# The up-projection of a ConvFFN: seven products of sums of quarters in place of eight

## The chip, the cores and the metric

The kernel runs on one core of one Trainium2 chip. A core has a tensor engine (TensorE, PE in the profile; its weight loads are shown as PEld), a vector engine (VectorE, DVE), a scalar engine (ScalarE, ACT), a general engine (GpSimd, POOL) and a queue that issues most of the DMAs (SyncE, SP). Each works through its own list of instructions in order and waits on semaphores for the others. The metric is the device time of one execution in microseconds (us); less is better.

## The reference

One inference step of a two-layer trunk. 1024 prompt tokens and 8 sequences of 4 sample tokens go through each layer: three kinds of linear-attention heads (RWKV-7, GLA, retention) side by side, an output projection, a LayerNorm, a gated ConvFFN, a second LayerNorm. All in float32; the states are outputs too. The part that matters here:

```python
def _conv_ffn(x, conv0, w_up, conv_w, conv_b, w_down):      # D_MODEL 1024, D_FF 2816, CONV_W 3
    t_ = x.shape[1]
    u = x @ w_up                                            # 1024 -> 2 * 2816
    buf = jnp.concatenate([conv0.astype(u.dtype), u], axis=1)
    c = conv_b + sum(conv_w[j] * buf[:, j:j + t_] for j in range(CONV_W))
    a, b = jnp.split(c, 2, axis=-1)
    return (jax.nn.gelu(a) * b) @ w_down, buf[:, -(CONV_W - 1):]
...
        x = _layer_norm(ALPHA * x + mix, ln1_g[l], ln1_b[l])
        f, cv = _conv_ffn(x, s_conv[l], ffn_up[l], ffn_conv_w[l], ffn_conv_b[l], ffn_down[l])
        x = _layer_norm(ALPHA * x + f, ln2_g[l], ln2_b[l])
```

Each of the 5632 columns of `u` has its own filter over three tokens; a column of the first half, after a GELU, multiplies its partner in the second half.

## The kernel before, in words

Channels lie on the 128 partitions, tokens along the free axis. The 1056 tokens are three blocks (`NB`): 384 and 384 of the prompt, and a third of 288, which holds the 32 sample tokens and the last 256 of the prompt.

A product in float32 is made of three matmuls in the type float32r (`mm3`): every operand is split in a high part (a cast on ScalarE) and a low part (the rest, by a subtraction on GpSimd or VectorE), and high x high, high x low and low x high are added up in PSUM. `split` (L188) makes the two parts; all matmuls have line L128. Their order on TensorE is that of the program; on the other engines the framework's scheduler sets the order when the kernel is built, by priority and its own estimate of time.

In the FFN stage (L1355 to L1505) `x1` is the normed input, 8 tiles of 128 channels (k), in two parts, by block. The 2816 columns of each half make `NJ` = 22 tiles; `j` and `j + 22` belong together.

- `up(j)` takes both tiles, one after the other, over the three blocks. For each tile and block 8 k x 3 matmuls go to a PSUM bank `pu` (pool `pg`, 3 banks). `up_conv` then copies the bank to `u` in SBUF (L1380), with two columns of halo from the block before (L1376, L1378; GpSimd), starts `c` from the same bank on ScalarE (L1392) and adds two taps on VectorE (L1401). For the third block the samples, with their old state, are treated apart (L1384 to L1390).
- `up_gate` makes the GELU (L1406), the product (L1407) and its two parts `hh`, `hl` (L188).
- `up_blocks` is the same for j = 0 and j = 21, block by block.
- After two j (a pair) `downs` multiplies both with their rows of the down weights: for each block and each of 8 output tiles m, 2 x 3 matmuls to a bank `pd` (pool `pd`, 5 banks), which VectorE adds to `acc` in SBUF (L1448). The first two groups also bring in the residual, once for the high and once for the low part of `x1` (L1451).
- The last pair's downs go block by block (`last_downs`), with the sums of the second LayerNorm beside them; layer 0's blocks 1 and 2 are normed beside the next layer's first products.

Weights come in pieces of 128 x 512 (256 KB): a DMA on SP's queue to a raw tile `wr`, then `split` to `wh` and `wl`. The pool `wp` is open for the whole kernel: 4 raw tiles, and 4 of each part for the input, output and up-projection weights; the down weights' parts have 4 tiles each in the FFN's own pool. The constants `cs` are loaded once, at the start. `x1` of a block is read by `pu` until the last j.

## Time and profile before

| | |
|---|---|
| median of 3 runs | 3429.16 us (3426.34 to 3441.1) |
| span of the profiled execution | 3430.9 us, the time it is taken by here |
| TensorE busy | 3198.4 us (93%) |
| VectorE / ScalarE / GpSimd busy | 2068.6 / 1434.7 / 1332.6 us |
| mean granted clock of TensorE | 0.952 |
| FFN stage of layer 0, first `pu` to the start of the next layer's | 929.1 to 1705 us |
| FFN stage of layer 1 | 2624 to 3431 us |

In the profile's groups a row has the line, the engine, the operation, the tiles written and read (buffer numbers left out), their shapes, the count, then the busy time and the mean of one, then the idle time of the engine just before and what ended it. In a timeline a row has the start, the length, the engine, the line, the operation, and in brackets how long the engine had been idle and for whom it waited. "wU8h" is the high part of the up weights of tile 8, "wD8l" the low part of the down weights of j = 8.

### The profile page before, as it was taken

What the parts mean: (1) busy time and instruction counts of PE and PEld (TensorE: products, weight loads), DVE (VectorE), ACT (ScalarE), POOL (GpSimd) and SP (SyncE); (2) the same over time, 40 slices, a digit from 0 to 9 for tenths busy, and PEclk for the clock granted to TensorE, in tenths of its full rate; (3) what the DMA queues carried; (4) which work ended last, traced back from release to release, by engine and by line L of the source; (5) the groups of instructions that cost most, each with busy time, mean ns of one, the idle gap of its engine ahead of it and who ended that gap; (6) DMA issues with size and microseconds to landing.
All of it is one profiled execution on the core that took longest, in us unless ns stands there. A gap on an engine that the chain in (4) does not pass through costs nothing.

```text
span 3430.9 us, 59397 instructions
## 1 busy us (share of the span) xinstructions
PE 3198.4 (93%) x22110; PEld 2975.9 (87%) x22110; DVE 2068.6 (60%) x5037; ACT 1434.7 (42%) x3208; POOL 1332.6 (39%) x1660
## 2 busy tenths in 40 slices
PE   9889999988899999999888999999788999999995
PEld 8778888776799999999877888887777999999995
DVE  3577565776756544454746866646777564545457
ACT  6554332334543334333575543323346423333335
POOL 5443222224553334333565522221336433433345
PEclk9789999998999999999998999999989999999998
DMA  7333213433311111111154432234433111111111
GB/s 249 112 110 99 79 54 102 139 115 102 106 60 47 44 44 50 50 44 50 56 164 140 133 91 68 63 128 119 129 94 100 48 44 44 56 44 44 44 44 56
DMA packets 233261, 288.24 MB, mean 84 GB/s; under 512 B 65212, under 2 KB 146908, under 8 KB 232972
## 3 DMA queue, kind: packets, MB, share of 16 engines
q1 hardware_dynamic: 223852, 271.98, 26.3%
q10 hardware_dynamic: 9120, 12.47, 1.2%
q8 instruction: 173, 2.83, 0.4%
q14 instruction: 116, 0.95, 0.1%
HBM read 225.94 MB, written 58.43 MB: 83 GB/s over the span
## 4 chain that ended last, share of the span: by engine, by line
PE 70%; DVE 16%; DMA 4%; ACT 4%; issue 3%; POOL 2%; SPq 1%; ACTq 0%; DVEq 0%; POOLq 0%
PE pu L128 27%; PE pd L128 13%; PE gt L128 9%; PE pa L128 5%; PE po L128 3%; DVE tm L630 2%; DVE U L632 2%; PE zy L128 2%; PE gps L128 2%; PE rop L128 1%; DVE c L1401 1%; PE gop L128 1%; POOL wil L188 1%; DMA N<-gd 1%; DVE s L940 1%
## 5 line engine op out<-in xcount | busy, mean ns | idle before, releaser
L1401 DVE SCALAR_TENSOR_TENSOR c<-u,ppt,c 128x32 f32<-128x32 f32 (+1 forms) x704 | 395.8, 589 | 545.5 <-ACT c L1392 523.8
L188 POOL TENSOR_TENSOR wil<-wir,wih 128x512 fp32r<-128x512 f32 (+1 forms) x264 | 366.3, 1395 | 365.8 <-ACT wih L188 361.2
L128 PE MATMUL gt<-wih,xh 128*128 128x320 f32 (+1 forms) x1008 | 340.1, 339 | 0.9 <-DVE mx L388 0.9
L1448 DVE TENSOR_TENSOR acc<-acc,pd 128x384 f32<-128x384 f32 (+1 forms) x480 | 247.7, 518 | 139.5 <-PE pd L128 137.5
L128 PE MATMUL gt<-wil,xh 128*128 128x320 f32 (+1 forms) x1008 | 316.1, 315 | 6.5 <-POOL wil L188 5.2
L128 PE MATMUL gt<-wih,xl 128*128 128x320 f32 x896 | 281.6, 314 | 0.0
L188 ACT CAST wih<-wir 128x512 fp32r<-128x512 f32 (+1 forms) x296 | 185.6, 637 | 162.4 <-PE po L128 71.5
L128 PE MATMUL pa<-xh,wih 128*128 128x384 f32 (+1 forms) x576 | 216.5, 376 | 20.4 <-DVE mx L388 11.8
L630 DVE TENSOR_TENSOR tm<-U,N 96x60 f32<-96x60 f32 (+24 forms) x558 | 179.1, 321 | 69.9 <-DMA N<-gd 48.4
L128 PEld LDWEIGHTS gt<-wih,xh 128*128 128x128 f32 (+1 forms) x1008 | 187.5, 186 | 38.6 <-issue 21.9
L128 PE MATMUL pa<-xl,wih 128*128 128x384 f32 (+1 forms) x576 | 201.4, 350 | 3.3 <-POOL xl L188 3.0
L128 PE MATMUL pa<-xh,wil 128*128 128x384 f32 (+1 forms) x576 | 200.7, 348 | 3.6 <-POOL wil L188 2.2
L128 PEld LDWEIGHTS gt<-wil,xh 128*128 128x128 f32 (+1 forms) x1008 | 188.5, 187 | 10.2 <-POOL wil L188 9.1
L188 POOL TENSOR_TENSOR hl<-c,hh 128x384 fp32r<-128x384 f32 x132 | 128.1, 971 | 159.6 <-ACT hh L188 133.0
L632 DVE TENSOR_TENSOR U<-U,tm 96x60 f32<-96x60 f32 (+24 forms) x558 | 170.3, 305 | 14.0
L128 PEld LDWEIGHTS gt<-wih,xl 128*128 128x128 f32 x896 | 173.1, 193 | 0.0
L1392 ACT ACTIVATE c<-pu,ppt 128x384 f32<-128x384 f32 (+1 forms) x264 | 172.8, 655 | 0.0
L1380 ACT COPY u<-pu 128x384 f32<-128x384 f32 x176 | 84.1, 478 | 195.2 <-PE pu L128 195.1
L188 ACT CAST hh<-c 128x384 fp32r<-128x384 f32 x132 | 64.4, 488 | 222.4 <-DVE c L1407 222.3
L128 PEld LDWEIGHTS pa<-xh,wih 128*128 128x128 f32 x576 | 119.7, 208 | 35.1 <-DVE mx L388 13.2
L128 PE MATMUL po<-yh,wih 128*128 128x384 f32 (+1 forms) x384 | 138.9, 362 | 9.1 <-DVE ac L1325 6.7
L128 PE MATMUL po<-yh,wil 128*128 128x384 f32 (+1 forms) x384 | 131.7, 343 | 3.7 <-DVE wil L188 3.7
(810 smaller groups left out, 9862.6 us busy)
## 6 DMA issues: line engine op xcount, KB each, us to landing
wir<-in_wA_dram SPq DMA_DIRECT2D x144, 256.0 KB
wir<-in_wO_dram SPq DMA_DIRECT2D x96, 256.0 KB
wir<-in_wB_dram SPq DMA_DIRECT2D x56, 320.0 KB
tokd<-ev SPq DMA_DIRECT2D x112, 160.0 KB
x<-rkvd SPq DMA_DIRECT2D x16, 576.0 KB
tk<-tokd SPq DMA_DIRECT2D x16, 480.0 KB
rkvd<-mx SPq DMA_DIRECT2D x36, 192.0 KB
tk<-tokd SPq DMA_DIRECT2D x16, 400.0 KB
```

The costliest lines, as they stand in the source:

```text
L128: self.order(self.engine.matmul(out, lhsT, rhs, start=start, stop=stop), cols, 4 if rhs.dtype == F32 else 1)
L188: return A.copy(dst_h, src), (le or G).tensor_tensor(dst_l, src, dst_h.bitcast(F32), ALU.subtract)
L630: V.tensor_tensor(tm, U[:, 0:nr, i:i + 1].to_broadcast([4 * ns, nr, 31 - i]), N[:, i:i + 1, i + 1:32].to_broadcast([4 * ns, nr, 31 - i]), ...
L632: V.tensor_tensor(U[:, 0:nr, i + 1:32], U[:, 0:nr, i + 1:32], tm, ALU.add)
L940: self.ends["V"] = V.tensor_tensor(self.s1, acc[0] if k == 1 else self.s1, acc[k], ALU.add)
L1380: A.copy(u[:, 2:386], ps)
L1392: A.activation(c[:, :W], ps, AF.Identity, scale=pc(PP_CV + 4 * t + 2), bias=pc(PP_CV + 4 * t + 3))
L1401: V.scalar_tensor_tensor(cv, src, pc(PP_CV + 4 * t + tap), cv, ALU.mult, ALU.add)
L1448: V.tensor_tensor(acc[n][m], acc[n][m], ps, ALU.add)
```

## The change

For j = 1 to 21 the first two blocks are no longer multiplied tile by tile. Quarters are formed: the two tiles j and j + 22 by the two halves of k (weights `a11`, `a12`, `a21`, `a22`), and the two halves of k by the two blocks (`x1`). Sums of quarters are made on both sides, and seven products of a weight quarter or sum with an input quarter or sum (4 k x 3 matmuls of 384 columns each) are added up to the four results on VectorE (a variant of Strassen's scheme). The sums of `x1` are made once in each layer, beside j = 0 (`sums`: eight additions of high and low part into `acc`, sixteen differences, each split in two parts), the sums of weights in each `up` (four on VectorE, in place in the raw tiles). The results stand in `u` tiles in SBUF, from where the convolution takes them. The third block is multiplied as before, its products placed between the seven; for j = 21 (`late`) they come last, with the weights loaded and split again. j = 0 is done without the scheme.

The downs take the weights in halves of four output tiles, over all blocks for each. For blocks 0 and 1 the residual is the sum that `sums` has put in `acc`, so their second residual operation goes.

Pools: the mixers' weights, the constants `cs`, and `pbt` are in pools that are opened for a layer's mixers and closed before its FFN (`cs` is loaded in each layer, in layer 1 by ScalarE's queue). The FFN has its own weight pool `wf`: 5 raw tiles and 6 of each part, for up and down weights together. `u` has 6 tiles in place of 4, the first tile's `c` 3 in place of 4. The sums of the LayerNorms take the place of the sums of `x1`.

```diff
+FW, FR = 6, 5
-    wp = pool("wp")
-    cs = cp.tile([P, NCS], F32, name="cs")
+    cf = cp.tile([P, P + 6], F32, name="cf")
...
+        mstk, rstk = ExitStack(), ExitStack()
+        wp = pool(f"wp{l}", stack=mstk)
+        mp = pool(f"mp{l}", stack=mstk)
+        cs = mp.tile([P, NCS], F32, name="cs")
...
+        q.dma_start(cs, cst)
...
         gstk.close()
+        mstk.close()
...
+        wf = pool(f"wf{l}", stack=fstk)
...
+        def raw_piece(ap, name):
+            r = wf.tile([P, 512], F32, tag="wr", name=f"{name}r", bufs=FR)
+            nc.sync.dma_start(r.rearrange("p (a b) -> p a b", a=4), ap)
+            return r
+        def piece(raw, name):
+            p = [wf.tile([P, 512], F32R, tag=t, name=f"{name}{t}", bufs=FW) for t in ("wh", "wl")]
+            split(p[0], p[1], raw)
+            return [tuple(x[:, i * P:(i + 1) * P] for x in p) for i in range(4)]
...
+        def sums():
+            (h0, l0, _), (h1, l1, _) = x1[:2]
+            t2, t3, t4 = ([jp.tile([P, 4, 384], F32R, tag="tq", name=f"{n}{p}", bufs=6) for p in "hl"] for n in ("t2", "t3", "t4"))
+            def two(h, lo, raw):
+                A.copy(h, raw)
+                V.tensor_tensor(lo, raw, h.bitcast(F32), ALU.subtract)
+            for k in range(4):
+                for n, m, e in ((0, k, V), (1, k, V), (1, k + 4, G), (0, k + 4, G)):
+                    h, lo = x1[n][0][:, m].bitcast(F32), x1[n][1][:, m].bitcast(F32)
+                    e.tensor_tensor(acc[n][m], h, lo, ALU.add)
+                r11, r12, r21, r22 = acc[0][k], acc[1][k], acc[0][k + 4], acc[1][k + 4]
+                d1, d2, d3, d4 = (fp.tile([P, 386], F32, tag="u", name="d", bufs=6)[:, 0:384] for _ in range(4))
+                V.tensor_tensor(d3, r22, r12, ALU.subtract)
+                V.tensor_tensor(d1, r12, r11, ALU.subtract)
+                V.tensor_tensor(d2, r22, d1, ALU.subtract)
+                V.tensor_tensor(d4, r21, d2, ALU.subtract)
+                for h, lo, d in ((t2[0][:, k], t2[1][:, k], d2), (h1[:, k], l1[:, k], d1), (t3[0][:, k], t3[1][:, k], d3), (t4[0][:, k], t4[1][:, k], d4)):
+                    two(h, lo, d)
+            return [(h0[:, 0:4], l0[:, 0:4]), (h0[:, 4:8], l0[:, 4:8]), (h1[:, 4:8], l1[:, 4:8]), (h1[:, 0:4], l1[:, 0:4]), t2, t3, t4]
+        def product(ps, w, x, first=True, last=True):
+            for k in range(4):
+                mm3(ps, w[k][0], w[k][1], x[0][:, k], x[1][:, k], first and k == 0, last and k == 3)
+        def bank(n, name):
+            return (pg.tile([P, 512], F32, tag="g", name=name) if n == 2 else pd.tile([P, 512], F32, tag="d", name=name))[:, :NB[n][1]]
...
+                hs.append(up_gate(cs, n))
+                if n == 1:
+                    qs = sums()
+            return hs, qs
...
+        def up(j, qs, late=False):
+            b11, b21, b22, q1, q2, q3, q4 = qs
+            t0, t1 = j, j + NJ
...
+            r11, r12, r21, r22 = (raw_piece(wu(t, half), f"wU{t}") for t in (t0, t1) for half in range(2))
+            pa = bank(0, "pa")
+            w = piece(r11, "a11")
+            product(pa, w, b11)
+            u22 = new_u()
+            A.copy(u22[:, 2:386], pa)
+            if not late:
+                p0, p1 = bank(2, "p0"), bank(2, "p1")
+                product(p0, w, x2[0], True, False)
+            w = piece(r12, "a12")
+            if not late:
+                product(p0, w, x2[1], False, True)
+                c20, u20 = conv_samples(t0, 0, p0)
+            p2 = bank(0, "pg")
+            product(p2, w, b21)
...
+            V.tensor_tensor(v11, v22, p2, ALU.add)
+            c11 = conv_prompt(t0, 0, u11, v11)
+            if not late:
+                product(p1, piece(r21, "a21"), x2[0], True, False)
+            s1 = wf.tile([P, 512], F32, tag="wr", name="s1r", bufs=FR)
+            V.tensor_tensor(s1, r21, r22, ALU.add)
+            V.tensor_tensor(r21, r11, r21, ALU.subtract)
+            V.tensor_tensor(r11, s1, r11, ALU.subtract)
+            V.tensor_tensor(r12, r12, r11, ALU.subtract)
+            pb_ = bank(0, "pb")
+            product(pb_, piece(r11, "s2"), q2)
...
+            V.tensor_tensor(v12, v22, pb_, ALU.add)
+            p5 = bank(0, "pc")
+            product(p5, piece(s1, "s1"), q1)
+            p7 = bank(0, "pf")
+            product(p7, piece(r21, "s3"), q3)
+            V.tensor_tensor(v22, v12, p7, ALU.add)
+            V.tensor_tensor(v12, v12, p5, ALU.add)
+            p4 = bank(0, "pd")
+            w = piece(r22, "a22")
+            product(p4, w, q4)
...
+            V.tensor_tensor(v21, v22, p4, ALU.add)
+            V.tensor_tensor(v22, v22, p5, ALU.add)
+            halo(u22, 1, u21)
+            hs = [up_gate((c11, conv_prompt(t1, 1, u21, v21)), 0)]
+            if not late:
+                product(p1, w, x2[1], False, True)
+                c21, u2 = conv_samples(t1, 1, p1)
+                conv_rest(t1, c21, u2, u22)
+            p3 = bank(0, "pe")
+            product(p3, piece(r12, "s4"), b22)
+            V.tensor_tensor(v12, v12, p3, ALU.add)
+            halo(u12, 1, u11)
+            c12 = conv_prompt(t0, 0, u12, v12)
+            hs.append(up_gate((c12, conv_prompt(t1, 1, u22, v22)), 1))
+            if late:
+                for t, half, p in ((t0, 0, 0), (t0, 1, 0), (t1, 0, 1), (t1, 1, 1)):
...
+                    product(ps, whole(wu(t, half), f"wU{t}"), x2[half], half == 0, half == 1)
...
+            else:
+                conv_rest(t0, c20, u20, u12)
+            hs.append(up_gate((c20, c21), 2))
             return hs
...
+            a = acc[n][m]
+            if n == 2 and group < 2:
...
+            elif group:
+                V.tensor_tensor(a, a, ps, ALU.add)
+            else:
+                V.scalar_tensor_tensor(a, a, ALPHA, ps, ALU.mult, ALU.add)
+        def downs(j, hs, group):
+            for half in range(2):
+                ws = [whole(wd(j + i, half), f"wD{j + i}") for i in range(2)]
+                for n in range(3):
+                    for m in range(4):
+                        down(4 * half + m, n, group, hs, [w[m] for w in ws])
...
+        hs_ = up(NJ - 2, qs)
+        hs = up(NJ - 1, qs, True)
...
+        ws = [sum((whole(wd(NJ - 2 + i, half), f"wD{NJ - 2 + i}") for half in range(2)), []) for i in range(2)]
+        last_downs(0, hs)
         last_downs(1, hs)
```

More of the change, by code (lines that the diff above doesn't have):

```diff
@@ L1402, in up_conv, with taps, conv_start @@
-            return c[:, :W], u
+            else:
+                o = 48 if n == 2 else 0
+                G.tensor_copy(u[:, o:o + 2], prev[:, 384:386])
+        def taps(t, c, uu, cv, w):
+            for tap in (1, 0):
+                V.scalar_tensor_tensor(cv, uu[..., tap:tap + w], pc(PP_CV + 4 * t + tap), cv, ALU.mult, ALU.add)
+        def conv_start(t, i, src, W):
+            c = fp.tile([P, 384], F32, tag=f"c{i}", name="c", bufs=3 if i == 0 else 2)[:, :W]
+            A.activation(c, src, AF.Identity, scale=pc(PP_CV + 4 * t + 2), bias=pc(PP_CV + 4 * t + 3))
+            return c
@@ new lines, in product, with up_blocks @@
+        def product(ps, w, x, first=True, last=True):
[3 more added lines that the diff above has]
+            return (pg.tile([P, 512], F32, tag="g", name=name) if n == 2 else pd.tile([P, 512], F32, tag="d", name=name))[:, :NB[n][1]]
+        def up_blocks(j):
+            w = [[whole(wu(j + i * NJ, half), f"wU{j}") for half in range(2)] for i in range(2)]
+            prev, hs, qs = [None] * 2, [], None
@@ L1430, in up_blocks @@
             for n in range(3):
-                if n == 2:
-                    between(hs)
                 cs = []
                 for i in range(2):
-                    c, prev[i] = up_conv(j + i * NJ, i, n, w[i], prev[i])
+                    t = j + i * NJ
+                    ps = bank(2, f"pu{t}")[:, :NB[n][1]] if n == 2 else pg.tile([P, 512], F32, tag="g", name=f"pu{t}")[:, :384]
+                    for half in range(2):
+                        hf = slice(4 * half, 4 * half + 4)
+                        product(ps, w[i][half], (x1[n][0][:, hf], x1[n][1][:, hf]), half == 0, half == 1)
```

173 lines of the change are left out of this document (85 added, 88 removed).

## The prediction

> **What bounds the kernel now.** I read the page first, then the busy time of each engine by window, then TensorE's rows in order of time, then the groups of instructions by shape. The page gives the span and the busy time of each engine:
>
> ```profile
> span 3430.9 us, 59397 instructions
> ...
> PE 3198.4 (93%) x22110; PEld 2975.9 (87%) x22110; DVE 2068.6 (60%) x5037; ACT 1434.7 (42%) x3208; POOL 1332.6 (39%) x1660
> ```
>
> A share of the whole span hides the stages. The ConvFFN stage, the one that changes, is read from a window of exactly two pairs of j (each pair: two up-projections, then their down-projections). Columns: window, length, then busy time of PE, PEld, DVE, ACT, POOL, the granted clock, DMA share, GB/s.
>
> ```profile
> 1163.30:1301.50 138.20, 138.20 (x867) 138.20 (x866) 68.84 (x125) 49.00 (x104) 53.12 (x85) 1.00 0.15 47
> ```
>
> TensorE is busy all the time at full clock; nobody keeps it waiting. So a matmul taken away here is time taken away, as long as its new inputs come in time. One pair takes 138.2 / 2 = 69.1 us, in which VectorE is busy 34.4 us, ScalarE 24.5 us, GpSimd 26.6 us.
>
> The price of a matmul is its pitch (start to start), not its duration, as they overlap. The two rows below stand 12 matmuls of 384 columns apart; the next two stand 22 matmuls of 288 columns apart (in the output projection):
>
> ```profile
> 1099.78 0.33 PE L128 MATMUL pu<-x1h,wU5l 128*128 128x384 f32 x1
> ...
> 1101.86 0.33 PE L128 MATMUL pu<-x1h,wU5l 128*128 128x384 f32 x1
> ```
>
> ```profile
> 915.26 0.30 PE L128 MATMUL po<-yh,wih 128*128 128x288 f32 x1
> ...
> 918.18 0.29 PE L128 MATMUL po<-yl,wih 128*128 128x288 f32 x1
> ```
>
> So 12 of 384 take 2.08 us (0.173 each), and one of 288 takes 2.92 / 22 = 0.133 us. An up-projection of before is 96 x 0.173 + 48 x 0.133 = 23.0 us, and the downs of a pair 23.0 us too; 3 x 23.0 = 69.0 agrees with the window.
>
> **The change part by part.**
>
> *1. Fewer matmuls.* One product is 4 k-tiles x 3 matmuls = 12 matmuls of 384. Each j from 1 to 21 needs seven in place of eight: 2.08 us less, 21 j in 2 layers: 42 x 2.08 = **-87.4 us**. The third block, j = 0 and the downs keep their matmuls. A pair goes to 64.9 us.
>
> *2. More work for VectorE, GpSimd and ScalarE.* The durations, from the groups of one window that holds the work of two pairs (busy us, mean ns):
>
> ```profile
> L1401 DVE SCALAR_TENSOR_TENSOR c<-u,ppt,c 128x384 f32<-128x384 f32 x32 | 20.2, 630 | 42.8 <-ACT c L1392 42.3
> L1448 DVE TENSOR_TENSOR acc<-acc,pd 128x384 f32<-128x384 f32 x32 | 17.7, 552 | 11.3 <-PE pd L128 11.1
> ...
> L1401 DVE SCALAR_TENSOR_TENSOR c<-u,ppt,c 128x256 f32<-128x256 f32 x16 | 9.7, 606 | 0.0
> L1407 DVE TENSOR_TENSOR c<-c 128x384 f32<-128x384 f32 x8 | 8.4, 1046 | 0.3
> ...
> L1380 ACT COPY u<-pu 128x384 f32<-128x384 f32 x16 | 7.7, 479 | 20.2 <-PE pu L128 20.2
> ...
> L1401 DVE SCALAR_TENSOR_TENSOR c<-u,ppt,c 128x32 f32<-128x32 f32 x16 | 6.5, 408 | 9.6 <-ACT c L1392 9.6
> ...
> L188 POOL TENSOR_TENSOR wU8l<-wU8r,wU8h 128x512 fp32r<-128x512 f32 x2 | 2.7, 1356 | 1.6 <-ACT wU8h L188 1.4 <-ACT u L1386 0.2
> ...
> L1407 DVE TENSOR_TENSOR c<-c 128x288 f32<-128x288 f32 x4 | 1.8, 453 | 0.1
> ...
> L188 ACT CAST wU8h<-wU8r 128x512 fp32r<-128x512 f32 x2 | 1.2, 620 | 0.5 <-PE pu L128 0.4
> ```
>
> Per up-projection come seven additions of a PSUM bank to an SBUF tile, which are like `acc<-acc,pd`: 7 x 0.55 = 3.9 us; four sums of weight pieces (512 wide, all in SBUF); and four more splits of pieces: 4 x 0.62 us on ScalarE, 4 x 1.36 us on GpSimd. Three copies of 0.48 us leave ScalarE. The nearest rows to a weight sum are two of VectorE's own 512-wide subtractions:
>
> ```profile
> 913.20 1.76 DVE L188 TENSOR_TENSOR wil<-wir,wih 128x512 fp32r<-128x512 f32 x1
> ...
> 918.56 0.68 DVE L188 TENSOR_TENSOR wil<-wir,wih 128x512 fp32r<-128x512 f32 x1
> ```
>
> 0.68 to 1.76 us; I take 1.0, nearer the undisturbed one. Per pair: VectorE 34.4 + 7.7 + 8.0 = 50.1, GpSimd 26.6 + 10.9 = 37.5, ScalarE 24.5 + 5.0 - 2.9 = 26.6 us, against 64.9 of TensorE. By busy time all fit under the matmuls, so I cost this work at nothing inside the up-projections; if its cover is gone, the price is the third rival's.
>
> *3. The start of the downs.* Before, an up-projection ends with the third block, and the downs begin with 24 x 2 matmuls of block 0 (8.3 us), then block 1 as long: the gated values have much room. After it the weights go in halves, so each block's downs are 24 matmuls (4.15 us), and block 0's and 1's values hang on the last products. Their chain, from the rows of one tile on ScalarE, VectorE and GpSimd:
>
> ```profile
> 1179.62 0.68 ACT L1392 ACTIVATE c<-pu,ppt 128x384 f32<-128x384 f32 x1
> 1182.23 0.51 ACT L188 CAST hh<-c 128x384 fp32r<-128x384 f32 x1 [1.93 <-DVE c L1407]
> ```
>
> ```profile
> 1180.34 1.27 DVE L1401 SCALAR_TENSOR_TENSOR c<-u,ppt,c 128x384 f32<-128x384 f32 x2 [2.45 <-ACT c L1392]
> 1181.64 0.56 DVE L1407 TENSOR_TENSOR c<-c 128x384 f32<-128x384 f32 x1
> ...
> 1185.87 1.53 DVE L1407 TENSOR_TENSOR c<-c 128x384 f32<-128x384 f32 x1
> ```
>
> ```profile
> 1182.83 1.01 POOL L188 TENSOR_TENSOR hl<-c,hh 128x384 fp32r<-128x384 f32 x1 [2.63 <-ACT hh L188]
> ...
> 1185.52 3.04 POOL L188 TENSOR_TENSOR wU30l<-wU30r,wU30h 128x512 fp32r<-128x512 f32 x2 [1.38 <-ACT wU30h L188]
> ```
>
> From 1179.62 to 1183.84 (1182.83 + 1.01): 4.22 us; with the addition of `pd` (0.55) and about 0.26 us until its last matmul has drained (an estimate: its 0.33 us record less the pitch, and a hop), `hl` of block 0 stands 5.03 us after the start of the matmuls that follow product `pd`. TensorE has until then half of `p1` (12 x 0.133 = 1.6), `pe` (2.08), three matmuls of the first j and one of the second (0.69): 4.35 us. So it waits **0.7 us** at least. The upper bound: the second row of `c<-c` shows 0.97 us more for the same operation while GpSimd runs a split; three such hits on the two chains of blocks 0 and 1 give 3.6 us. I take 1.5 (one hit, partly hidden), as VectorE has three quarters of its time filled. Behind the waiting matmul stands all of TensorE. There are 20 such starts (the last two j have the third block's late products as cover): **+30 us** (14 to 72). No gain is possible here, as nothing waits there now.
>
> *4. The sums of x1 in j = 0.* `sums` must have `t2` ready before `pb` of j = 1. TensorE's cover after block 1 of j = 0 is block 2 (48 x 0.133 = 6.4 us) and `pa`, `p0`, `pg`, half of `p1` (2.08 + 3.2 + 2.08 + 1.6 = 8.9): 15.3 us. VectorE's bill: 32 operations on SBUF of 384 (four differences and four low parts for each of four k) at 0.56 = 17.9 us, and its first taps are late already:
>
> ```profile
> 944.84 4.43 DVE L1401 SCALAR_TENSOR_TENSOR c<-u,ppt,c 128x384 f32<-128x384 f32 x6 [6.16 <-POOL u L1376]
> ```
>
> ```profile
> L128 PEld LDWEIGHTS pu<-x1h,wU1h x48: 187/188/188, 954.0 to 2660.3; 128*128 128x128 f32 x48
> ```
>
> j = 1 starts at 954.0, so block 1 ended at 947.6 and `pb` would be due at 962.9. From 944.8 VectorE needs 6.1 us for the taps and products of blocks 0 and 1 undisturbed (8 x 0.62 + 2 x 0.56), then 17.9, of which the last two operations aren't `t2`'s: 967.7, or 4.8 us late, and 7 with two hits of 0.97. With every second one of the 32 hit by a GpSimd instruction (16 x 0.97 = 15.5) and some 5 us for the sums' eight additions on GpSimd, queued among its splits: about 25 us. I take 14 in each layer: **+28 us** (14 to 50). The eight VectorE additions of high and low parts lie in its idle 6.16 us above.
>
> *5. Pools by stage.* The mixers' weight pool of layer 1 now takes space that the last downs of layer 0 still read, so its first splits can't be made early; and `cs` (some 820 KB) is read a second time, in ScalarE's queue, behind whatever frees its space and ahead of what ScalarE does next. The row in question:
>
> ```profile
> 1705.21 0.45 PE L128 MATMUL pa<-xh,wih 128*128 128x384 f32 x1 [0.32 <-ACT xh L188]
> ...
> 1708.92 0.45 PE L128 MATMUL pa<-xl,wih 128*128 128x384 f32 x1 [0.50 <-POOL xl L188]
> ```
>
> The first matmul of layer 1 then waits for one cast and one split (0.62 + 1.36 = 2 us), and up to four more splits (5.4 us) fall where GpSimd already sets the pace: 2 to 8, I take **+5 us**. In layer 0 nothing moves. The weights' loads on SP have one buffer more than before and each piece is held longer, till its sum is split; the last is free when `pe` begins, 2.08 us before the next j, whose matmuls on that piece start 3.7 us in, so they cost nothing; a late load would hold up those queued behind it on SP. The late j reads its four pieces twice, under 6 us of products; the second residual operation that blocks 0 and 1 lose is VectorE's and hidden.
>
> Sum: -87.4 + 30 + 28 + 5 = -24 us, 3430.9 - 24 = 3407. The profiled span lies 1.7 above the median of the runs (3429.16), so in their terms **3405 us**.
>
> **The rivals.**
>
> *The covers hold.* All at the low ends: -87.4 + 14 + 14 + 2 = -57, or 3372. For it: 50 of 65 us on VectorE leave room. Against it: 16 us of that is new and comes in the up-projections alone.
>
> *The short waits cost clock.* The clock falls after a long idle time:
>
> ```profile
> 914.00:919.00 5.00, 3.46 (x24) 3.22 (x24) 5.00 (x7) 2.68 (x7) 3.00 (x4) 1.00 0.42 132
> 923.00:932.00 9.00, 4.54 (x12) 3.97 (x13) 6.97 (x14) 3.49 (x6) 2.71 (x3) 0.50 0.28 91
> ```
>
> ```profile
> 927.46 1.33 PE L128 MATMUL lnm<-s,cs 128*128 128x288 f32 x2 [6.57 <-DVE s L940]
> ```
>
> After 6.57 us idle it stood at 0.50 until past 932, some 5 us of matmuls, so 2.5 us lost; waits of about 1 us inside the first window left it at 1.00. If every start of the downs did it: 20 x 2.5 = +50, or 3455. The Trainium skill (TensorE: Matmul & The Clock Gate, HAM oscillation) puts the limit at gaps above some 3.4 us; by that rule waits of 1.5 us cost no clock, and the trace agrees for 1 and 6.57 us.
>
> *GpSimd and VectorE shut each other out.* The `c<-c` of 1.53 us ended only after the split beside it, and `acc<-acc,pd` keeps its 552 ns. If VectorE's work on two SBUF inputs (per pair (20.2 + 9.7 + 8.4 + 6.5 + 1.8) / 2 = 23.3, with the weight sums 31.3) and GpSimd's 37.5 us can't overlap at all, a pair needs 68.8 us, and its matmuls no longer set it: the rival decides once this sum passes 64.9. With the 1.5 us of the downs a pair costs +1.2: 18 full pairs +22, the six other j keep -12, two first downs +3, the sums at their upper end +50, layer 1 +5: +68, or 3497. Against it: parts of each instruction did overlap (the split of 3.04 us for two began before the taps ended). The Trainium skill (GPSIMD Engine Reference, Key points) says that GpSimd shares its SBUF interfaces with VectorE and contends with instructions that have two SBUF inputs; the trace agrees, 1.53 against 0.56 us, and this is the rule that speaks against the change.
>
> **How the numbers follow.** Forecast 0.40 (its own range 3385 to 3430), covers hold 0.20, clock 0.12, shut out 0.28. A change under 0.5% (17 us: 3412 to 3446) can't be told from none. Faster: 0.20 and 0.25 of the forecast's 0.40: 0.45. Same: the forecast's other 0.15, and 0.05 each of clock and shut out in part: 0.25. Slower: 0.07 + 0.23 = 0.30. The range 3355 to 3495 leaves about 0.05 below and 0.13 above.
>
> **What would show it.** The pair's window: 64.9 us of matmuls plus waits of TensorE ahead of `pd` on `hl`; a wait of some 14 us on `t2` ahead of `pb` in j = 1; weight sums near 1.0 us; the clock at 1.00 between. Wrong: waits ahead of products on the pieces' low parts in every j (third rival), a clock of 0.50 in the stage (second), or no wait at all.

## The result and the profile after

The changed kernel takes 3644.76 us (median of 4 executions, 3639.55 to 3654.0), the kernel before, run beside it, 3435.13 (3426.34 to 3444.05): a ratio of 1.061, 95% interval 1.058 to 1.064. It is about 210 us slower; the prediction was 3405, with 3495 as its upper end.

The first lines of the page of the changed kernel, to be read against those of before:

```profile
span 3637.8 us, 59686 instructions
...
PE 3210.8 (88%) x21606; PEld 2963.4 (81%) x21606; DVE 2451.7 (67%) x5547; ACT 1503.3 (41%) x3288; POOL 1645.5 (45%) x1852
```

TensorE issues 504 matmuls less (42 x 12, as reckoned) and yet is busy 12 us longer: its matmuls ran slower, and it stood idle besides. The windows of two pairs, cut at the start and the end of each downs (the columns are those of the prediction's windows: length, busy time of PE, PEld, DVE, ACT, POOL, granted clock, DMA share, GB/s), say where:

```profile
1149.80:1303.90 154.10, 139.15 (x818) 136.81 (x817) 100.28 (x168) 53.66 (x108) 77.89 (x100) 0.92 0.13 42
...
1149.80:1183.00 33.20, 26.86 (x146) 25.82 (x145) 24.49 (x45) 7.87 (x16) 9.53 (x12) 0.85 0.02 8
1183.00:1225.00 42.00, 42.00 (x267) 42.00 (x266) 25.48 (x39) 18.96 (x39) 29.40 (x38) 1.00 0.23 70
1225.00:1262.00 37.00, 28.39 (x146) 27.09 (x145) 24.83 (x45) 7.93 (x16) 9.54 (x12) 0.82 0.03 8
1262.00:1303.90 41.90, 41.90 (x265) 41.90 (x265) 25.48 (x39) 18.90 (x39) 29.42 (x38) 1.00 0.21 70
```

The two up-projections of a pair take 42.0 us with no idle time at full clock; before they took 46.1. There the change does what it says. All the loss of this window lies in the downs, 33.2 and 37.0 us for work that took 23.0. Cut in the same way, the whole difference of the two spans (206.9 us) is: the ups between the downs, 18 x -4.1 = -74; the 20 downs, 697 in place of 464, +233; the first two j of each layer, up to their downs, +27 and +21; all the rest -1.

One start of the downs, as TensorE's rows show it (start, duration, operation; in brackets the idle time ahead and what ended it), and the stretches of that downs:

```profile
1155.83 0.69 PE L130 MATMUL pd<-hh,wD5wh 128*128 128x384 f32 x1 [5.29 <-ACT hh L187]
1157.55 0.69 PE L130 MATMUL pd<-hl,wD5wh 128*128 128x384 f32 x1 [1.03 <-POOL hl L187]
```

```profile
1149.80:1155.80 6.00, 0.74 (x5) 0.42 (x3) 5.16 (x8) 3.08 (x7) 3.25 (x6) 0.78 0.00 0
1155.80:1158.00 2.20, 1.14 (x2) 0.74 (x3) 2.20 (x5) 0.86 (x2) 1.82 (x3) 0.50 0.00 0
1158.00:1166.00 8.00, 7.99 (x32) 7.66 (x32) 6.31 (x13) 2.37 (x5) 1.78 (x2) 0.66 0.00 0
1166.00:1183.00 17.00, 17.00 (x110) 17.00 (x110) 10.82 (x21) 1.57 (x3) 2.68 (x2) 1.00 0.05 16
```

TensorE does three matmuls of the first j and then waits 5.29 us for `hh` of the second, and 1.03 for its `hl`; after that the clock is at 0.50 for some microseconds of matmuls. Why `hh` is late stands on VectorE's list, the product `pd` having ended before 1146.4 (TensorE's next product starts at 1146.18):

```profile
1144.90 0.56 DVE L1540 TENSOR_TENSOR u<-u,pc 128x384 f32<-128x384 f32 x1
1150.32 0.69 DVE L1526 TENSOR_TENSOR s1r<-wU28r 128x512 f32<-128x512 f32 x1 [4.86 <-DMA wU28r<-in_wU_dram]
1150.93 0.55 DVE L1547 TENSOR_TENSOR u<-u,pd 128x384 f32<-128x384 f32 x1
1151.51 0.56 DVE L1548 TENSOR_TENSOR u<-u,pc 128x384 f32<-128x384 f32 x1
1152.32 2.45 DVE L1398 SCALAR_TENSOR_TENSOR c<-u,ppt,c 128x384 f32<-128x384 f32 x3 [0.25 <-ACT c L1402]
1154.69 0.55 DVE L1432 TENSOR_TENSOR c<-c 128x384 f32<-128x384 f32 x1
```

The scheduler has put the first weight sum of the *next* j (L1526) ahead of the addition of `pd` (L1547). The sum waits 4.86 us for its load, and VectorE with it; the addition comes 4.6 us late. GpSimd's list shows a second, smaller delay, two splits of the next j ahead of `hl` (`hh` is done at 1155.78, `hl` starts 0.54 us later):

```profile
1152.92 1.26 POOL L187 TENSOR_TENSOR a11wl<-wU6r,a11wh 128x512 fp32r<-128x512 f32 x1 [0.61 <-ACT u L1416]
...
1154.77 1.58 POOL L187 TENSOR_TENSOR a12wl<-wU6r,a12wh 128x512 fp32r<-128x512 f32 x1
1156.32 1.17 POOL L187 TENSOR_TENSOR hl<-c,hh 128x384 fp32r<-128x384 f32 x1
```

The first of the two loads of that row was issued only when a split of the down weights had freed one of the five raw buffers (the split ends at 1146.19):

```profile
1144.89 1.30 POOL L187 TENSOR_TENSOR wD5wl<-wD5r,wD5wh 128x512 fp32r<-128x512 f32 x1 [1.09 <-ACT wD5wh L187]
```

```profile
1146.22 1.57 SPq L1367 DMA_DIRECT2D wU28r<-in_wU_dram  x2
```

The other loss, in the first two j of layer 0:

```profile
945.13 0.69 PE L130 MATMUL pu<-x1h,wU0wh 128*128 128x384 f32 x1 [3.77 <-ACT c L1402]
985.19 0.61 PE L130 MATMUL p<-x1h,a21wh 128*128 128x288 f32 x1 [20.48 <-ACT c L1402]
```

The long wait is not at `pb` on `t2`, but one product earlier: `p1` needs a PSUM bank that still holds block 2 of j = 0. Its copies and the start of its convolution, which free the bank, stand on ScalarE's list behind the casts of the sums, and those wait for VectorE's differences:

```profile
983.78 0.51 ACT L1445 CAST t2h<-d 128x384 fp32r<-128x384 f32 x1 [1.36 <-DVE d L1455]
...
984.54 0.61 ACT L1402 ACTIVATE c<-pu,ppt 128x288 f32<-128x288 f32 x1
```

By the kernel's text the differences `d` also take their tiles from the six of `u`, ahead of block 2's own `u`. Whether the list or these tiles held the copies back was not tried. The short wait, in j = 0, is not the sums': j = 0 takes 31.7 us in the changed kernel, 31.8 in kernel 1 below, which has no differences, and 31.8 in kernel 7, which makes the sums a j later; 25.0 before. There ScalarE's copies of block 0 stand behind block 2's LayerNorm.

### The profile page after: what moved, and what is told of

The parts are those of the page before. It is cut to its first block, busy times and chain, and to the rows that moved or that the text cites. A ratio compares the mean times of both kernels' runs of the same rounds, so it can differ in the third digit from the quotient of the medians.

```text
span 3637.8 us, 59686 instructions
## 1 busy us (share of the span) xinstructions
PE 3210.8 (88%) x21606; PEld 2963.4 (81%) x21606; DVE 2451.7 (67%) x5547; ACT 1503.3 (41%) x3288; POOL 1645.5 (45%) x1852
## 5 line engine op out<-in xcount | busy, mean ns | idle before, releaser
L1398 DVE SCALAR_TENSOR_TENSOR c<-u,ppt,c 128x32 f32<-128x32 f32 (+2 forms) x704 | 517.0, 768 | 168.7 <-ACT c L1402 154.5
L187 POOL TENSOR_TENSOR hl<-c,hh 128x384 fp32r<-128x384 f32 x132 | 145.7, 1107 | 144.4 <-ACT hh L187 144.4
L1402 ACT ACTIVATE c<-u,ppt 128x384 f32<-128x384 f32 x168 | 116.8, 707 | 217.5 <-DVE u L1547 135.2
L130 PEld LDWEIGHTS pa<-xh,wih 128*128 128x128 f32 x576 | 121.0, 210 | 34.5 <-DVE mx L380 10.6
L130 PE MATMUL po<-yl,wih 128*128 128x384 f32 (+1 forms) x384 | 130.0, 339 | 0.0
L130 PEld LDWEIGHTS pa<-xl,wih 128*128 128x128 f32 x576 | 122.0, 212 | 9.5 <-POOL xl L187 6.3
```

The source lines that it names most:

```text
L130: self.order(self.engine.matmul(out, lhsT, rhs, start=start, stop=stop), cols, 4 if rhs.dtype == F32 else 1)
L187: return A.copy(dst_h, src), (le or G).tensor_tensor(dst_l, src, dst_h.bitcast(F32), ALU.subtract)
L1398: V.scalar_tensor_tensor(cv, uu[..., tap:tap + w], pc(PP_CV + 4 * t + tap), cv, ALU.mult, ALU.add)
L1402: A.activation(c, src, AF.Identity, scale=pc(PP_CV + 4 * t + 2), bias=pc(PP_CV + 4 * t + 3))
```

## The experiments

Two theories ran through all of them. One (theory 1 in the first texts on record, Q in the later ones): what costs the time is the order, what stands ahead in the queues at the start of the downs and how little TensorE has to do meanwhile. The other (theory 2, later W): it is the amount of work on VectorE and GpSimd, which hold each other up. Beside them stood the question what the half clock behind the waits costs (theory 3). The table gives every kernel's time against the kernel before, and the window of two pairs, from the third to the fifth start of the downs in layer 0 (for the kernel before, the window of the prediction); idle is the window less PE's busy time, as in the windows above.

| kernel | us, median | ratio to before (95%) | two pairs, us | idle, us | clock |
|---|---|---|---|---|---|
| before | 3435 | | 138.2 | 0 | 1.00 |
| changed | 3644.8 | 1.061 (1.058 to 1.064) | 154.1 | 15.0 | 0.92 |
| 1 scheme undone | 3449.3 | 1.004 (1.002 to 1.005) | 138.4 | 0 | 1.00 |
| 2 filler ahead of the downs | 3603.1 | 1.049 (1.047 to 1.052) | 150.3 | 8.8 | 0.98 |
| 3 weight sum later | 3587.3 | 1.042 (1.039 to 1.046) | 148.2 | 12.1 | 0.97 |
| 4 late block 2 | 3533.0 | 1.028 (1.025 to 1.031) | 142.2 | 6.7 | 0.96 |
| 5 = 3, next splits later | 3583.7 | 1.043 (1.040 to 1.046) | 146.4 | 10.9 | 0.98 |
| 6 = 5, second half's splits and weight sum later | 3554.3 | 1.036 (1.032 to 1.039) | 143.2 | 7.7 | 0.98 |
| 7 = 6, j = 1 plain | 3529.4 | 1.028 (1.025 to 1.030) | 143.2 | 7.8 | 0.98 |
| 8 = 4 and 7, and more | 3549.2 | 1.033 (1.030 to 1.036) | 145.1 | 11.1 | 1.00 |
| 9 GpSimd's weight splits left out | 3530.5 | 1.028 (1.025 to 1.030) | 143.5 | 8.3 | 0.98 |
| 10 = 6 and 9 | 3492.4 | 1.017 (1.012 to 1.021) | 139.7 | 5.9 | 0.99 |
| 11 products ahead of the downs, and more | 3403.3 | 0.991 (0.988 to 0.995) | 130.2 | 0 | 1.00 |
| 12 products ahead of the downs alone | 3439.4 | 1.002 (1.000 to 1.004) | 133.1 | 2.4 | 1.00 |

**1. The scheme undone.** All j by `up_blocks`; the pools by stage, the halved down weights and the additions of high and low parts in j = 0 are kept (sixteen, eight on VectorE and eight on GpSimd; the section on the change counts eight), the differences of x1 and the weight sums are gone.

```diff
-                if j + i:
-                    hs.append(up(j + i, qs))
-                else:
-                    h, qs = up_blocks(0)
-                    hs.append(h)
+                hs.append(up_blocks(j + i)[0])
```

> Edit: the scheme undone, everything else of the change kept (pools by stage, down weights in halves, the residual from the sums of high and low parts): every j is multiplied block by block as j = 0 is, so eight products' worth of matmuls, no weight sums, no differences of x1. If the loss lies in the scheme's additions and their order: 3430 to 3460, the kernel before or a little above. If it lies in the pools or the halved downs: 3500 or more, with waits ahead of the downs.

3449.31 us, ratio 1.004: downs of 23.2 us with no wait. The halves and the pools cost next to nothing here; the 12.5 us that it takes more than the kernel before lie within what its first two j take more (56.1 us a layer against 48.0). So the loss hangs on the scheme, its sums and their order. One thing this run can't show: here block 2 ends the up-projection, and covers the gate. Whether whole down weights in the scheme, with 8.3 us of matmuls for block 0 in place of 4.15, would have hidden block 1's wait was not run.

**2. A filler ahead of the downs.** 24 matmuls of 288 columns (3.2 us) into a spare bank; nobody reads it.

```diff
         def downs(j, hs, group):
+            pw = bank(2, "warm")
+            for _ in range(24):
+                TE.matmul(pw, x1[0][0][:, 0, 0:P], x1[0][0][:, 0, 0:288], start=True, stop=True)
```

> Edit: 24 matmuls of 288 columns into a spare PSUM bank ahead of each pair's downs, their result unused (3.2 us of matmuls in a stretch where TensorE idles 5.4 us). Theory 3 (clock): a good part of what the downs lose is half clock after the idle time, 10 us at 0.5 in a downs of 35, so some 4 us in each of 20. If the matmuls keep the clock up, the downs fall to about 31 us and the time by 40 to 90 to 3555 to 3605. If the clock isn't a cost of its own: no change (3635 to 3655), or slower where the matmuls come ahead of the ready ones.

3603.06 us: 64 us of matmuls more (20 x 3.2), and yet 42 us faster than the changed kernel. The wait at the start shrinks by what the filler takes,

```profile
1143.62 0.45 PE L130 MATMUL pd<-hh,wD5wh 128*128 128x384 f32 x1 [2.20 <-ACT hh L187]
1145.34 0.69 PE L130 MATMUL pd<-hl,wD5wh 128*128 128x384 f32 x1 [1.27 <-POOL hl L187]
```

and the time at half clock over the two FFN stages falls from 305 to 194 us (the clock's rows, added up). The waits do cost clock, beside themselves. And work put there is nearly free, which is what the last two experiments use.

**3. The weight sum later.** The first weight sum is ordered behind the last addition (`v12 += p3`) of the up before.

```diff
-            V.tensor_tensor(s1, r21, r22, ALU.add)
+            TE.after(V.tensor_tensor(s1, r21, r22, ALU.add), lastv[0])
...
-            V.tensor_tensor(v12, v12, p3, ALU.add)
+            lastv[0] = V.tensor_tensor(v12, v12, p3, ALU.add)
```

> Edit: the first of the four weight sums of an up-projection is kept behind the last addition (of product pe) of the up-projection before it in VectorE's order; nothing else. Theory 1 (VectorE's queue): ahead of each downs VectorE stands at the next j's weight sum, which waits for its DMA, while the addition of product pd behind it has all it needs; that takes about 2.8 of the 5.4 us that TensorE idles. Then the wait ahead of the downs falls to about 2.6 us, with less time at half clock behind it, the downs of a pair go from 35 to 27 to 30 us, and the time to 3490 to 3560. Theory 2 (GpSimd and VectorE shut each other out and the chain is long by that): the order changes little, the wait stays above 4.5 us, the time above 3610.

3587.26: 57 us better, between the two expectations. The rows of the same start:

```profile
1144.83 0.44 PE L130 MATMUL pd<-hh,wD5wh 128*128 128x384 f32 x1 [1.74 <-ACT hh L187]
1148.52 0.69 PE L130 MATMUL pd<-hl,wD5wh 128*128 128x384 f32 x1 [3.25 <-POOL hl L187]
```

The wait on `hh` fell from 5.29 to 1.74, and the next one took its place: `hl`, 3.25 us behind, after the two splits on GpSimd.

**4. Block 2 late.** The second j of each pair uses the form that only the last two j had: block 2 in one piece after the last product, with the weights loaded and split again.

```diff
-                    hs.append(up(j + i, qs))
+                    hs.append(up(j + i, qs, i == 1))
```

> Edit: the second up-projection of each pair takes the form that j = 21 has: the third block's products come last, with their weights loaded and split again (four more loads and splits in each pair, one fewer for the sum a21). They give the chain from product pd to the downs 6.4 us more cover. Theory 1 and theory 3: the wait of 6.4 us ahead of the downs goes and with it the half clock; downs at 23 to 25 us, time 3400 to 3450, about the kernel before. Theory 2 in its strong form (a pair is bound by the sum of GpSimd's and VectorE's work on SBUF, to which 5.4 us of splits are added): TensorE waits elsewhere in the pair and the time stays above 3520.

3532.98, 112 us better, though it adds four loads and four splits a pair: block 0's gate has 6.4 us of matmuls more to hide behind. Still 2.41 us on `hh` and 0.95 on `hl` are left at the start. The expected 3400 to 3450 was missed. The time lies above the 3520 that the strong form of the second theory named, but TensorE's waits in the two pairs (6.7 us) all stand at the starts of the downs, and not elsewhere in the pair as that theory wanted.

**5 and 6. The queues ordered by hand.** In 5 the weight sum as in 3, and the splits `a11`, `a12` of the next pair behind `hl` of block 1. In 6 also the splits of the second half of the down weights, and the weight sum behind block 1's gate.

```diff
-            w = piece(r11, "a11")
+            w = piece(r11, "a11", hls[-2] if first else None)      # a12 likewise; 5 and 6
...
-                ws = [whole(wd(j + i, half), f"wD{j + i}") for i in range(2)]
+                ws = [whole(wd(j + i, half), f"wD{j + i}", hls[-2] if half else None) for i in range(2)]      # 6
```

> The first weight sum of each first up waits in VectorE's queue behind the last addition of the up before (as in the run that moved only this), and beside it the GpSimd halves of the splits a11 and a12 of the next pair wait behind the low part of h of block 1, so that both low parts of h stand ahead of them. In the run with only the first of these the low part of block 0 came 3.3 us after its high part, behind a11wl, two small copies and a12wl, and that was 3.26 of 5.0 us of idle time at each start of the downs. Theory Q (what costs the time at the downs is what stands ahead in the queues of VectorE and GpSimd): the 3.26 us fall to about 1, the low clock behind them shrinks to 3.4 us per downs or less, 20 x (2.3 + 1.7) = 80 us less than 3587: 3490 to 3530. Theory W (the additions, taps and splits at the end of the up are simply too much work for the time, whatever their order): another wait takes its place, 3565 or more.

> As the run before in this call, and beside it the splits of the second half of the down weights wait in GpSimd's queue behind the low part of h of block 1 (they are due only 12 us into the downs), and the first weight sum of the next pair stands behind the gate's multiplication of block 1. So GpSimd has no split between the last up's end and the low part of h but those of the first half, and the two taps of block 0, 1.62 us each beside the splits, should fall towards 0.63. Theory Q: h of block 0 is there at most 1 us after its first use, downs of 24 to 27 us in place of 34.9, 3450 to 3490. Theory W: downs still 30 us or more, 3560 or more.

5 took 3583.68, no better than 3: `hl` now follows `hh` by 0.64 us, but the wait moves to block 1 (1.50 and 0.83 us, where 3 had 0.85). That is what W had forecast. 6 took 3554.31, 33 us better than 3, between the two expectations and close to W's; TensorE's waits in one downs are

```profile
1419.40 0.44 PE L130 MATMUL pd<-hh,wD13wh 128*128 128x384 f32 x1 [0.42 <-ACT hh L187]
1420.70 0.45 PE L130 MATMUL pd<-hl,wD13wh 128*128 128x384 f32 x1 [0.86 <-POOL hl L187]
1426.91 0.44 PE L130 MATMUL pd<-hh,wD13wh 128*128 128x384 f32 x1 [1.94 <-ACT hh L187]
1427.98 0.45 PE L130 MATMUL pd<-hl,wD13wh 128*128 128x384 f32 x1 [0.64 <-POOL hl L187]
```

The splits that stood ahead on GpSimd and the weight sum on VectorE are gone, but the chain (addition, convolution, taps, GELU, product, cast, low part) still does not have the lists to itself. At block 0's start ScalarE casts the next pair's `a12` first, after a wait for the matmuls of `pe`; VectorE's product, the input of `hh`, had ended at 1418.21:

```profile
1418.32 0.62 ACT L187 CAST a12wh<-wU14r 128x512 fp32r<-128x512 f32 x1 [0.57 <-PE pe L130]
1418.84 0.51 ACT L187 CAST hh<-c 128x384 fp32r<-128x384 f32 x1
```

At block 1 VectorE does block 2's product (288 wide) ahead of block 1's, with additions to `acc` between:

```profile
1424.93 0.45 DVE L1434 TENSOR_TENSOR c<-c 128x288 f32<-128x288 f32 x1
...
1425.76 0.55 DVE L1434 TENSOR_TENSOR c<-c 128x384 f32<-128x384 f32 x1
```

And block 1's second `c` starts only when block 0's `hl` is done (ScalarE's row for it ends a wait of 0.70 us on `POOL hl`), which fits the two buffers of that tile; a third was not tried. So how late the chain would be with nothing else in the lists stays open.

**7. j = 1 plain.** As 6, with `up_blocks` for j = 0 and 1 and the sums after block 1 of j = 1.

> As the run before in this call, and the second column block (j = 1) is computed plainly too, with the sums of x1 behind the products of its block 1, so that the sums are first used 38 us later or more and nothing waits for their conversions. It gives up the saving of one block per layer (2 x 2.08 = 4.2 us) and should take away the waits of 20.6 and 14.2 us in j = 1 and most of the 6.7 and 6.8 in j = 0 that the sums had brought: 2 x (17 + 6 - 2) = 42 us less at most, 25 at least, than the run before. If the sums only moved their work under other work that then waits, the same or up to 10 us less.

3529.37, 25 us better, the low end. The 20 us wait is gone, but not the extra time of j = 0, which the text on record had put down to the sums: it still takes 31.8 us. The first downs come 57.0 us into layer 0 in place of 75.6; but the sums then run into them (39.9 us, 10 more than the others).

**8. Everything that then seemed to help.** 4 and 7, the taps of block 1 behind block 0's gate, and the sums in four parts spread over j = 0 and j = 1.

> All of it together: the second up of each pair does block 2 last and plainly (24 matmuls of 288 more after the last product of sums, its weights loaded again); the queue orders of the second run of the call before (weight sum behind the gate of block 1, the splits of the next pair and of the second half of the down weights behind the low part of h of block 1); the taps of block 1 behind the gate of block 0; j = 1 plain; and the sums of x1 cut into four parts, one after block 1 and one after block 2 of j = 0, one each after blocks 0 and 1 of j = 1, the first half of block 1's own differences made again there. Theory Q (order and cover, not the amount of work): downs of 23 to 25 us with no low clock, first downs at 48 to 54 us, so 3529 - 20 x 5 to 6 (downs) - 2 x 12 (first pair) = 3385 to 3420, below the kernel before. Theory W (work of VectorE and GpSimd, 24 us of splits and taps that shut each other out, is the bound at the end of each pair): downs still 27 us or more, 3460 or more.

3549.18: worse than 4 and 7 alone, W's outcome. With the reloaded pieces GpSimd has no gap: low parts of six pieces stand ahead of `hl`, five of them ahead of the halos, and VectorE, late with the taps of block 2, is late with the additions that free TensorE's banks:

```profile
1131.51 0.44 PE L130 MATMUL pd<-hl,wD5wh 128*128 128x384 f32 x1 [1.29 <-POOL hl L187]
1138.02 0.45 PE L130 MATMUL pd<-hh,wD4wh 128*128 128x384 f32 x1 [0.69 <-DVE acc L1608]
1140.67 0.45 PE L130 MATMUL pd<-hh,wD4wh 128*128 128x384 f32 x1 [1.32 <-DVE acc L1608]
```

**9 and 10. GpSimd's weight splits left out,** of the changed kernel and of 6.

```diff
-            split(p[0], p[1], raw)
+            A.copy(p[0], raw)
+            A.copy(p[1], raw)
```

> The changed kernel with GpSimd's share of the weight splits of the FFN left out: in place of the low part (raw minus high part, on GpSimd) ScalarE writes the raw piece once more, so that what is computed is no longer the reference's; the matmuls, loads and buffers are the same, GpSimd keeps only the low parts of h, the halos and small copies. ScalarE gets 28 casts of 0.6 us per pair more. The late weight sum ahead of the addition of p4 stays as it was. If the loss at the downs is GpSimd's work (its queue, and VectorE's operations that last longer beside it: taps 945 ns for 384 elements against 630), the downs fall from 34.9 to 27 us or less and the whole to 3490 or less, the taps to 650 ns or less. If it is only the weight sum that waits for its load ahead of the addition, the downs stay at 31 us or more and the whole at 3570 or more.

> The same left out of the kernel with the queue orders mended (weight sum behind the gate of block 1, later splits behind the low part of h), which took 3554 with 29.6 us per downs, 1.3 us of idle at block 0's start and 2.6 at block 1's. If GpSimd's splits and the taps beside them are what is left there: downs of 25 us or less, 3554 - 20 x 4.5 = 3465 or less. If what is left is the chain itself (convolution, gate, split one behind the other, and the two buffers of c), which does not need the splits: 3530 or more.

3530.51 and 3492.43: 114 and 62 us better, both between the expectations. A group of the same two-pair window tells how VectorE fares beside the splits. Changed kernel, then 9:

```profile
L1398 DVE SCALAR_TENSOR_TENSOR c<-u,ppt,c 128x384 f32<-128x384 f32 x32 | 30.2, 944 | 4.8 <-ACT c L1402 4.5
```

```profile
L1399 DVE SCALAR_TENSOR_TENSOR c<-u,ppt,c 128x384 f32<-128x384 f32 x32 | 19.4, 616 | 5.7 <-ACT c L1403 4.1 <-POOL u L1395 1.3
```

A tap of 384 takes 616 ns without the splits and 944 beside them. So the second theory has its part in the lateness. But with the splits gone from GpSimd *and* the queues in order (10), waits of 0.94 and 0.63 us at the start and 0.64 or more at block 1 remain. They aren't the chain's alone: ScalarE, which now makes both parts, does those of the next pair's `a12` ahead of `hh`, whose input was ready at 1131.53:

```profile
1131.87 0.61 ACT L1376 CAST a12wl<-wU6r 128x512 fp32r<-128x512 f32 x1
1132.39 0.51 ACT L187 CAST hh<-c 128x384 fp32r<-128x384 f32 x1
```

How much of 9's gain is a shorter queue and how much faster taps is not separated.

**11 and 12. Products of the next pair ahead of the downs.** `up` becomes a generator that stops once after its first product and block 2's first bank: 12 matmuls of 384 and 24 of 288, 4.8 us. That part is issued ahead of the downs of the pair before; the second row of weight pieces is loaded, and summed, after them.

```diff
-            r11, r12, r21, r22 = (raw_piece(wu(t, half), f"wU{t}") for t in (t0, t1) for half in range(2))
+            r11, r12 = (raw_piece(wu(t0, half), f"wU{t0}") for half in range(2))
...
             if not late:
                 product(p0, w, x2[1], False, True)
+            yield
+            r21, r22 = (raw_piece(wu(t1, half), f"wU{t1}") for half in range(2))
...
+            nxt = up_steps(j + 2, qs)
+            next(nxt)
             downs(j, hs, j // 2)
```

12 is this alone. 11 has beside it the orders of the weight sum and the second half's splits from 6, j = 1 plain with the sums in four parts as in 8, and the downs in the order of blocks 0, 2, 1.

> The mended queue orders (weight sum, second half's splits), j = 1 plain with the sums in four parts, and beside it the first product and block 2's first two half products of the next pair (12 matmuls of 384 and 24 of 288, 4.8 us) stand ahead of the downs of this pair in TensorE's order, and the downs take block 2 before block 1. So block 0's gate has 4.8 us more and block 1's 7.7 us more until TensorE needs them; nothing is loaded or split twice. If a wait at the start of the downs is only a matter of what TensorE has to do meanwhile: idle under 1 us per downs and no low clock, 23.5 us each, first pair 92 us in place of 105: 3554 - 20 x 5.5 - 2 x 14 = 3415, 3395 to 3440. If the work ahead only shifts the wait (the splits of a11 and a12 stand ahead of the low part of h again, or the second half's splits come late): 3480 or more.

> The changed kernel with one edit: the first product and block 2's first two half products of the next pair (4.8 us of TensorE) stand ahead of the downs, and its second row of weight pieces is loaded and summed only after the downs are laid down, so that the weight sum is put into VectorE's queue later too. The sums stay in j = 0, j = 1 keeps the scheme, no queue is ordered by hand, the downs keep the order of blocks 0, 1, 2. If the start of the downs needed only cover: downs of 23 to 25 us, first pair 75.6 + 4.8 + 24 to 29, and 3644 - 20 x 10.5 to 12 = 3405 to 3435. If the queue orders are needed beside it (the second half's splits ahead of the low part of h, taps that last longer beside them): the wait of block 1 stays, 26 to 29 us per downs, 3470 to 3540.

12 took 3439.38, 205 us less than the changed kernel and no different from before; 11 took 3403.3, faster than before by 0.9% (0.5 to 1.2). That this is near the forecast of 3405 is chance: 11 is another program, and its costs are not those of the forecast's sum. The two-pair window of 11, and then all of TensorE's waits that 12 has from its second j to the end of its first downs:

```profile
1121.40:1251.60 130.20, 130.20 (x819) 130.20 (x818) 100.91 (x170) 53.53 (x110) 79.87 (x100) 1.00 0.16 49
```

```profile
982.91 0.61 PE L130 MATMUL p<-x1h,a21wh 128*128 128x288 f32 x1 [20.40 <-ACT c L1402]
1009.84 0.44 PE L130 MATMUL pd<-hh,wD1wh 128*128 128x384 f32 x1 [0.77 <-ACT hh L187]
1010.92 0.44 PE L130 MATMUL pd<-hl,wD1wh 128*128 128x384 f32 x1 [0.64 <-POOL hl L187]
```

In this window of 11 a pair takes 65.1 us with no wait at all. VectorE and GpSimd are as busy as in the changed kernel (100.91 and 79.87 us of the window against 100.28 and 77.89), and the taps are as slow:

```profile
L1400 DVE SCALAR_TENSOR_TENSOR c<-u,ppt,c 128x384 f32<-128x384 f32 x33 | 32.5, 986 | 4.6 <-ACT c L1404 1.7 <-issue 1.4 <-POOL a12wl L187 0.6
```

That settles it for the full pairs: neither the amount of work nor its slowness costs time by itself. What cost it was that the chain from the last product to `h`, with what stood ahead of it in the lists, was on the path that sets the end, with 4.35 us of matmuls to hide it. 12 changes two things at once (TensorE's order, and with it the place of the second row's loads and sums). 3, which moves the first sum alone, brought 57 us, and 2 bears out that matmuls there shorten the wait; but the two gains need not add up, and the moved products with the sums left where they were is a run that was not made. 11's order of blocks (0, 2, 1) is also the one in which VectorE finishes them in 6. The 36 us between 12 and 11 were not taken apart: the downs lost 0.8 to 1.5 us of idle time each in 12 and none in 11, and the first pair 106.4 us in layer 0 against 97.9. In 11 that first pair still holds a wait of 3.60 us in j = 0, one of 2.77 in j = 1, and 6 us in its downs.

## Why the prediction was wrong

**Step 1 (-87.4) held.** The pair went from 69.1 to 65.1 us where nothing waits, 4.0 of the 4.2 reckoned.

**Step 2 (nothing inside the up-projections) held,** almost to the number: a pair keeps VectorE busy 100.28 / 2 = 50.1 us (50.1 reckoned), GpSimd 38.9 (37.5), ScalarE 26.8 (26.6), and the ups show no wait. That VectorE's total agrees is luck in part: the 32 taps of 384 alone keep it 5.0 us a pair longer ((30.2 - 20.2) / 2), the weight sums 2.5 less (0.69 us each, not 1.0), and other rows make up the rest.

**Step 3 (the start of the downs, +30, 14 to 72) failed.** It measured +233, 11.7 us a start in place of 1.5. The step followed a chain of operations as if every engine were free when its turn came, with one delay by a split. Three things were left out. First, what the scheduler sets ahead in the queues: the weight sum of the next j waiting for its load (3: 57 us), and the splits ahead of `hl`. Second, that it is two chains, block 1's behind block 0's on the same engines and tiles: in 6 the second wait is the longer one. Third, the clock: each of the 20 downs had 10.1 us at half clock on the mean. Of the 11.7 us a start, 7.7 are more idle time; the other 3.9 are matmuls that ran slower. And the lists stay mixed to the end: in 6 and 10 a cast of the next pair still stands ahead of `hh`. The step's own lower bound (4.35 us of matmuls against a chain of 5.03) should have warned: a chain that already fails to fit at its best grows by every delay, one for one.

**Step 5 failed at the raw pieces.** "The last is free when `pe` begins ... so they cost nothing" looked at the matmuls that use the piece. But the first user is a VectorE instruction, and behind it in VectorE's queue stood the addition on which the downs wait. The pools' own +5 was about right where it falls: layer 1's first matmul comes 3.14 us after the last downs in place of 0.32, and twenty matmuls on the lag is 6.4 us; after 575 matmuls 0.5 of it is left.

**Step 4 (the sums, +28, 14 to 50) was within its range and misplaced.** Against 20.9 us the j that first uses them took 22.7 more in layer 0 and 16.3 in layer 1: +39. VectorE's 32 operations kept it busy 27 and 20 us, 17.9 reckoned undisturbed; GpSimd's eight additions took 10.6 us, not 5. The wait came at a PSUM bank of block 2, one product earlier than `pb`, because block 2's convolution queued behind the sums' casts on ScalarE, an engine that the step does not look at. Beside it j = 0 took 6.7 and 6.8 us more, for which the sum has no term and which kernel 1 has as well. A part of that is only moved: from the last matmul of the output projection to the first `pu` it was 8.5 us before and is 5.2 and 5.6 now.

**The rivals.** "The covers hold" was wrong for this order of the program; in 11, which gives the cover and orders the queues, it is so for the full pairs. "Short waits cost clock" had the mechanism, with 2.5 us a start where 3.9 were lost. "GpSimd and VectorE shut each other out" did not decide as it was put: its sum, 31.3 + 37.5, passes a pair's matmul time, and yet 11 runs its pairs without a wait. They slow each other down, by half for a tap, which counts only where nothing covers. No rival had the case that came: on the path, an instruction that belongs to the next j, at the head of an in-order queue.

## What to carry to other kernels

Reckon a pipeline's seam by the list of each engine at that moment, not by the sum of busy times: write down what may be queued ahead of the first instruction of the chain, and what that in turn waits for (a load, a buffer). Where a saving on TensorE makes results appear later relative to their use, look for independent matmuls to put in between before mending queues: 4.8 us of the next pair's products, moved (and with them the loads and sums of its second row), brought 205 us, where orders by hand brought 90 and leaving out all of GpSimd's weight splits 114. Orders by hand have to reach every list: here they left out ScalarE's.

## What the hardware showed unexpectedly

**In these stages the clock follows slots of 3.41 us, and half a slot of idle time is enough to lower it.** The low clock comes in multiples of 3.4 us; in every trace here its edges lie on one grid of 3.413 us, to within 0.004 us. Cutting a trace at the edges of those rows gives slots; the first row below is the slot of a wait of 0.94 and 0.63 us in kernel 10, the second the slot after it, and the next four those of another downs of the same kernel, where the same two waits are divided by the edge of a slot and more idle time follows (3.66 us in all):

```profile
1130.94:1134.35 3.41, 1.84 (x10) 1.26 (x9) 3.33 (x8) 2.85 (x6) 1.36 (x2) 1.00 0.00 0
1134.35:1137.76 3.41, 3.41 (x12) 3.41 (x11) 3.41 (x8) 1.77 (x4) 0.14 (x1) 0.50 0.00 0
1199.20:1202.61 3.41, 2.64 (x16) 2.32 (x14) 3.09 (x8) 3.35 (x8) 0.73 (x3) 1.00 0.00 0
1202.61:1206.03 3.42, 2.62 (x13) 2.36 (x14) 3.34 (x7) 2.34 (x5) 1.19 (x2) 1.00 0.00 0
1206.03:1209.44 3.41, 2.08 (x13) 1.77 (x11) 3.31 (x6) 0.94 (x3) 1.10 (x1) 1.00 0.00 0
1209.44:1212.85 3.41, 2.65 (x13) 2.40 (x14) 2.10 (x5) 0.07 (x1) 1.17 (x3) 1.00 0.03 5
```

1.57 us of idle time in one slot is followed by a slot at 0.50; 1.33 us is not. Over the FFN stages of all fourteen traces, from the first `pu` to the end of the last downs (worked out from TensorE's rows and the clock's), none of some 5800 full-clock slots with less than 1.5 us idle was followed by a slow one, all 233 with over 2.0 us were, and between them 79 of 130. It is no limit for every kind of work: outside these stages, in the same traces, 79 slots with less than 1.5 us idle were followed by a slow one. The prediction drew on the Trainium skill (TensorE: Matmul & The Clock Gate, HAM oscillation) for a limit at gaps above some 3.4 us; these runs do not agree: two waits of together 1.6 us, in one slot, were enough. The Trainium skill (TensorE: Matmul & The Clock Gate, What's actually happening) speaks of a window of 3413 ns that runs freely; with that the rows agree. A grid that runs freely would also explain why the same wait cost clock in one pair and none in the next; no run here moves the waits against the grid and changes nothing else.

**A wait that is cut is not a wait that is gone.** The idle time in two pairs went 15.0, 12.1, 10.9, 7.7 us as one delay after another was taken from the queues (3, 5, 6): each removal gave back less than the wait it ended (in 3 the wait on `hh` fell by 3.55 us at the start shown, the idle time by 1.5 us a start), since the next link of the chain was nearly as late.
